# Layer 0's gate projection taken into the attention items by a written TensorE order, and layer 1's modulation sums in two parts

## The chip, the cores and the metric

One core of one Trainium2 chip runs the whole program. The metric is the device time of one execution in microseconds, the median of several runs; lower is better. The engines are TensorE (PE, its weight loads PEld), VectorE (DVE), ScalarE (ACT), GpSimd (POOL) and SyncE (SP, whose queue issues most of the DMAs).

## The reference, cut to what matters

Two layers, 128 context tokens and 512 latent tokens of width 2048. Layer 0 is grouped-query attention with 16 heads of 128 and 4 key/value heads, layer 1 an RG-LRU. Each mixer's output is multiplied by a SiLU gate of the branch's width before its output projection; each layer has a shift, a scale and a gate from `silu(cond) @ w_mod[l]`.

```python
def adaln(cond, w_mod, b_mod):
    m = jax.nn.silu(cond) @ w_mod + b_mod
    shift, scale, gate = jnp.split(m[:, None, :], 3, axis=-1)
    return shift, scale, gate
...
def attn_context(h, w_in, q_norm, k_norm, w_out):
    q, k, v, g = attn_in(h, w_in, q_norm, k_norm)
    o = blocked_attention(q, k, v)
    return (o * jax.nn.silu(g)) @ w_out, k, v
...
    for l in range(DEPTH):
        sh_c, sc_c, ga_c = adaln(c_ctx[None, :], w_mod[l], b_mod[l])
        sh_s, sc_s, ga_s = adaln(c, w_mod[l], b_mod[l])
        hp = rms_norm(y_p, g_pre[l]) * (1.0 + sc_c) + sh_c
        hs = rms_norm(y_s, g_pre[l]) * (1.0 + sc_s) + sh_s
        ...
        y_p = y_p + ga_c * rms_norm(mp, g_post[l])
        y_s = y_s + ga_s * rms_norm(ms, g_post[l])
```

Latent tokens attend to 768 keys (256 cached, 512 own), context tokens to their own 128.

## The kernel before

All large products are float32, split into a high and a low fp32r part (`split_w`: ScalarE casts `wh`, VectorE subtracts to get `wl`), and taken as three matmuls (`mm3`). The split weights live in a ring of three pairs, the raw weights in a pool of four 1 MB tiles (`rawp`). The layer's input stays in SBUF transposed, as `hi` and `lo`, 16 tiles of 644 columns (512 latent tokens, 2 spare, 128 context tokens, 2 spare).

The order of layer 0: first the input and V; then K and four blocks of Q (`gemm_nat`, 4 calls of the background each, then `norm_rope` on VectorE and ScalarE with a write to DRAM); then the gate in 8 blocks of two heads (`gemm_T`), whose result `g_evac` brings from PSUM with a tanh and a multiplication and writes to DRAM as `g_s`; then attention; then the output projection.

Attention runs over 72 items (h, m): for each head four blocks of 128 latent queries, and after every second head one item (h, 4) with the context queries of both. An item has a score part (`stage_s`: 6 matmuls 384 wide into a score tile of PSUM, then maximum, exp, normalization), a part that transposes the probabilities (`stage_t`: 6 transposes and their split into `pth` and `ptl`), and after every second item the product with V (`stage_v`: 18 matmuls). A loop issues the score part of item n, the transposes of item n−3, the product of item n−4 and a piece of the next head's q (`step_q`). There are two score tiles, four probability tiles and two of `pth` and `ptl`. Queries come back from DRAM together with the gate, the product with V is multiplied by the gate and goes straight into `hi` and `lo` for the output projection.

Layer 1's shift and scale come from `gemv`: VectorE multiplies rows of `w_mod` with the conditioning, one column of it per partition, and adds into two accumulators (`ga`, one each for latents and context). It is a generator. Part 0 is the shift, part 1 the scale, each has two halves of 1024 columns, and a half has 8 steps of four sums. Each half ends in a final: split, 8 matmuls with `sel` 512 wide, a copy, 8 transposes. `background()` in each of 36 calls (20 in K/Q, 16 in the gate) adds 32/36 to a credit and takes a step when it has reached one.

A scheduler orders the instructions of each engine by priority in the order of the program, `split_w` ahead of others.

Of the kernel before, what the change touches and what calls it, by code (L numbers as in the profile page):

```python
# [9 lines left out]
F32 = mybir.dt.float32  # L10
# [7 lines left out]
D = 2048  # L18
# [15 lines left out]
AHEAD = 3  # L34
QV = (1, 2, 3)
QO = (2, 2, 3)
PB = 4
# [7 lines left out]
def hybrid_step(ctx: ExitStack, tc: tile.TileContext, i, o):  # L45
# [18 lines left out]
    g_s = [tc.dram_tile([128, TW], F32, name=f"g_s{h}") for h in range(NH)]  # L64
# [314 lines left out]
    def gemv():  # L379
        for part in range(2):  # L380
            for half in range(2):
                acc = [pb.tile([128, 1024], F32, name=f"ga{c}", tag=f"ga{c}") for c in range(2)]
                for kb in range(8):
                    w = rawp.tile([128, 2048], F32, name="raw", tag="raw")
                    w2 = w.rearrange("p (k n) -> p k n", k=2)
                    SY.dma_start(w2, i["w_mod"][1, kb * 256:kb * 256 + 256,
                                                part * D + half * 1024:part * D + half * 1024 + 1024]
                                 .rearrange("(k p) n -> p k n", p=128))
                    for k2 in range(2):
                        k = kb * 2 + k2  # L390
                        for c in range(2):
                            if k == 0:
                                V.tensor_scalar(acc[c], w2[:, k2], cT[:, k, c:c + 1], None, op0=mult)
                            else:
                                V.scalar_tensor_tensor(acc[c], w2[:, k2], cT[:, k, c:c + 1], acc[c],  # L395
                                                       op0=mult, op1=add)
                    yield
                pd_ = psd()
                for c in range(2):
                    ah, al = split_w(acc[c])  # L400
                    for j, x in enumerate((ah, al)):
                        for b in range(2):
                            PE.matmul(pd_[:2, b], sel[:, c], x[:, b * 512:b * 512 + 512], start=(c + j == 0),
                                      stop=(c + j == 2))
                row = pb.tile([2, 2, 512], F32, name="row", tag="row")
                S.copy(row, pd_[:2])
                for k in range(8):
                    PE.transpose(pd_[:, 0, 2 * k:2 * k + 2], row[:, k // 4, (k % 4) * 128:(k % 4) * 128 + 128],
                                 ident[:2, :2])
                kt = half * 8  # L410
                src = pd_[:, 0, :16].rearrange("p (k c) -> p c k", c=2)
                bcol = VA[:, 80 + part * 16 + kt:80 + part * 16 + kt + 8].unsqueeze(1).to_broadcast([128, 2, 8])
                if part == 0:
                    V.tensor_tensor(shift[1][:, kt:kt + 8].rearrange("p k c -> p c k"), src, bcol, op=add)
                else:
                    tmp = small.tile([128, 2, 8], F32, name="gt", tag="gt")
                    V.tensor_tensor(tmp, src, bcol, op=add)
                    gp = VA[:, 16 + kt:16 + kt + 8].unsqueeze(1).to_broadcast([128, 2, 8])
                    V.scalar_tensor_tensor(scale[1][:, kt:kt + 8].rearrange("p k c -> p c k"), tmp, 1.0,
                                           gp, op0=add, op1=mult)  # L420

    gv = gemv()
# [64 lines left out]
    def g_evac(acc, gb):  # L487
        for f in range(2):
            th = pb.tile([128, 2, 512], F32, name="qs", tag="qs", bufs=2)
            gg = pb.tile([128, 2, 512], F32, name="qf", tag="qf", bufs=2)  # L490
            S.activation(th[:, :, :TH], acc[f][:, :, :TH], AF.Tanh, scale=0.5)
            V.scalar_tensor_tensor(gg[:, :, :TH], th[:, :, :TH], 1.0, acc[f][:, :, :TH], op0=add, op1=mult)
            G.dma_start(g_s[gb * 2 + f].rearrange("p (h t) -> p h t", h=2), gg[:, :, :TH])

# [12 lines left out]
    for gb in range(8):  # L507
        g_evac(gemm_T(w_in, 3072 + gb * 256, background), gb)
# [10 lines left out]
    psS = pool("psS", 2, PSUM, stack=xs)  # L519
    psH = pool("psH", 4, PSUM, stack=xs)  # L520

    def pst():
        return psS.tile([128, 2, 512], F32, name="sp", tag="sp")
# [4 lines left out]
    def attn_kv(j):  # L528
        c = slice(j * 128, j * 128 + 128)
        raw = rawp.tile([128, 2048], F32, name="raw", tag="raw")  # L530
        kx = raw[:, :896].rearrange("p (t d) -> p t d", d=128)
        vx = pc_.tile([128, 7, 128], F32, name="vx", tag="vx")
        for x, cache, scr in ((kx, "cache_k", k_s), (vx, "cache_v", v_s)):
            SY.dma_start(x[:, 0:2], i[cache][0, 0, :, j, :].rearrange("(t p) d -> p t d", p=128))
            SY.dma_start(x[:, 2:7], scr[:, c].rearrange("(t p) d -> p t d", p=128))
        kh = pc_.tile([128, 896], F32R, name="kh", tag="kh", bufs=2)
        kl = pc_.tile([128, 896], F32R, name="kl", tag="kl", bufs=2)
        for a, e in ((0, 4), (4, 7)):
            p = psh()
            n = (e - a) * 128  # L540
            for t in range(a, e):
                PE.transpose(p[:, (t - a) * 128:(t - a) * 128 + 128], kx[:, t], ident)
# [3 lines left out]
        return kh, kl, vx  # L546

    def attn_v(j):
        kh, kl, vx = kvs[j]
# [5 lines left out]

    def attn_q(h):

        raw = rawp.tile([128, 2048], F32, name="raw", tag="raw")
        qx = raw[:, :640].rearrange("p (t d) -> p t d", t=5)
        SY.dma_start(qx, q_s[:, h * 128:h * 128 + 128].rearrange("(t p) d -> p t d", p=128))  # L560
        gt = raw[:, 640:640 + TW]
        SY.dma_start(gt, g_s[h])
        qh = ring.tile([128, 1024], F32R, name="wh", tag="wh")
        ql = ring.tile([128, 1024], F32R, name="wl", tag="wl")
        qs_[h] = qh, ql, gt, raw[:, 640 + TW:640 + TW + 512], qx

    def attn_qt(h, a, e):
        qh, ql, _, _, qx = qs_[h]
        p = psh()
        for m in range(a, e):  # L570
            PE.transpose(p[:, (m - a) * 128:(m - a) * 128 + 128], qx[:, m], ident)
        d = slice(a * 128, e * 128)
        n = (e - a) * 128
        S.copy(qh[:, d], p[:, :n])
        V.tensor_tensor(ql[:, d], p[:, :n], qh[:, d].bitcast(F32), op=sub)

    def softmax(sv, n, P, eng):
# [8 lines left out]
        for j in range(n):  # L586
# [3 lines left out]
            elif eng == "p":  # L590
# [454 lines left out]
```

## Time and profile before

| | |
|---|---|
| median of 3 runs | 1954.91 us (1953.88 to 1956.12) |
| profiled execution | 1955.32 us, span 1953.6 us |
| TensorE busy | 1883.5 us, 96% of the span |
| weight loads | 1673.2 us, 86% |
| VectorE busy | 1323.9 us, 68% |
| ScalarE busy | 865.0 us, 44% |
| DMA | 304.20 MB, mean 156 GB/s |

Busy time is what an engine's instructions took; matmuls are pipelined, so a busy TensorE may still lose time between them. The page names the engine that is busy longest, windows of the span tell in which stage the others have room, and the timeline at the borders of the stages tells what one stage hands to the next. Times in the rows below are microseconds from the start of the span.

### The profile page before, as it was taken

What the parts mean: (1) busy time and instruction counts of PE and PEld (TensorE: products, weight loads), DVE (VectorE), ACT (ScalarE), POOL (GpSimd) and SP (SyncE); (2) the same over time, 40 slices, a digit from 0 to 9 for tenths busy, and PEclk for the clock granted to TensorE, in tenths of its full rate; (3) what the DMA queues carried; (4) which work ended last, traced back from release to release, by engine and by line L of the source; (5) the groups of instructions that cost most, each with busy time, mean ns of one, the idle gap of its engine ahead of it and who ended that gap; (6) DMA issues with size and microseconds to landing.
All of it is one profiled execution on the core that took longest, in us unless ns stands there. A gap on an engine that the chain in (4) does not pass through costs nothing.

```text
span 1953.6 us, 26764 instructions
## 1 busy us (share of the span) xinstructions
PE 1883.5 (96%) x10857; PEld 1673.2 (86%) x10857; DVE 1323.9 (68%) x1846; ACT 865.0 (44%) x1255; POOL 133.1 (7%) x212
## 2 busy tenths in 40 slices
PE   4999999999999899999999989899999999999996
PEld 1567887879999899998888889899999999987885
DVE  3237759758375389998857774875685675798645
ACT  4441223222121388881223565666456456742232
POOL 0000000000000001110000000110010010020000
PEclk9999999999999999999999999999999999999998
DMA  9996535536454212225636673323232232546445
GB/s 342 343 318 209 166 109 183 178 123 200 149 178 158 74 38 74 74 97 174 204 130 211 226 263 109 122 77 117 94 102 92 94 100 64 175 140 212 146 149 216
DMA packets 194892, 304.20 MB, mean 156 GB/s; under 512 B 7232, under 2 KB 124608, under 8 KB 191952
## 3 DMA queue, kind: packets, MB, share of 16 engines
q1 hardware_dynamic: 188800, 276.20, 42.6%
q0 software_dynamic: 5968, 26.28, 3.7%
q8 instruction: 85, 1.39, 0.3%
q14 instruction: 39, 0.32, 0.0%
HBM read 273.03 MB, written 29.43 MB: 155 GB/s over the span
## 4 chain that ended last, share of the span: by engine, by line
PE 83%; DVE 6%; ACT 5%; issue 2%; DMA 2%; SPq 1%; POOL 0%; DVEq 0%; ACTq 0%; POOLq 0%
PE pd L184 22%; PE pd L185 22%; PE pd L186 22%; PE pd L215 2%; PE pm L276 2%; PE pd L217 2%; PE pd L218 2%; PE ph L631 1%; PE pg L184 1%; ACT L937 1%; PE pg L186 1%; PE pg L185 1%; PE sp L184 1%; PE sp L186 1%; PE ph L184 1%
## 5 line engine op out<-in xcount | busy, mean ns | idle before, releaser
L179 ACT CAST wh<-raw 128x1024 fp32r<-128x1024 f32 x248 | 258.1, 1048 | 604.8 <-PE pd L186 323.6
L180 DVE TENSOR_TENSOR wl<-raw,wh 128x1024 fp32r<-128x1024 f32 x248 | 301.4, 1221 | 237.5 <-ACT wh L179 236.6
L184 PE MATMUL pd<-wh,hi 128*128 128x512 f32 x1040 | 410.4, 395 | 5.8 <-ACT pd L783 3.3
L185 PE MATMUL pd<-wl,hi 128*128 128x512 f32 x1040 | 409.9, 394 | 0.0
L186 PE MATMUL pd<-wh,lo 128*128 128x512 f32 x1040 | 409.7, 394 | 0.0
L184 PE MATMUL pd<-hi,wh 128*128 128x322 f32 x1280 | 399.2, 312 | 0.0
L186 PE MATMUL pd<-hi,wl 128*128 128x322 f32 x1280 | 397.0, 310 | 1.1 <-DVE wl L180 1.1
L185 PE MATMUL pd<-lo,wh 128*128 128x322 f32 x1280 | 397.5, 311 | 0.0
L186 PEld LDWEIGHTS pd<-hi,wl 128*128 128x128 f32 x1280 | 241.6, 189 | 1.6 <-DVE wl L180 1.6
L185 PEld LDWEIGHTS pd<-lo,wh 128*128 128x128 f32 x1280 | 242.2, 189 | 0.1
L184 PEld LDWEIGHTS pd<-hi,wh 128*128 128x128 f32 x1280 | 241.4, 189 | 0.5 <-ACT wh L179 0.3
L184 PEld LDWEIGHTS pd<-wh,hi 128*128 128x128 f32 x1040 | 195.5, 188 | 52.5 <-ACT pd L783 3.7
L186 PEld LDWEIGHTS pd<-wh,lo 128*128 128x128 f32 x1040 | 195.4, 188 | 45.9
L185 PEld LDWEIGHTS pd<-wl,hi 128*128 128x128 f32 x1040 | 195.4, 188 | 45.4 <-DVE wl L180 0.3
L741 DVE SCALAR_TENSOR_TENSOR ga<-raw,cT,ga 128x512 f32<-128x512 f32 x256 | 175.5, 744 | 15.2 <-DMA ga<-b_mod 12.4
L395 DVE SCALAR_TENSOR_TENSOR ga<-raw,cT,ga 128x1024 f32<-128x1024 f32 x120 | 149.7, 1278 | 28.1 <-DMA raw<-w_mod 27.5
L215 PE MATMUL pd<-hi,wh 128*128 128x256 f32 (+1 forms) x256 | 80.5, 314 | 6.4 <-ACT wh L179 4.7
L184 PE MATMUL pd<-xh,wh 128*128 128x322 f32 x256 | 81.1, 318 | 5.2 <-ACT xh L875 4.4
L185 PE MATMUL pd<-xl,wh 128*128 128x322 f32 x256 | 80.0, 313 | 0.0
L218 PE MATMUL pd<-hi,wl 128*128 128x256 f32 (+1 forms) x256 | 79.9, 312 | 0.0
L217 PE MATMUL pd<-lo,wh 128*128 128x256 f32 (+1 forms) x256 | 79.8, 312 | 0.0
L186 PE MATMUL pd<-xh,wl 128*128 128x322 f32 x256 | 79.8, 312 | 0.0
(233 smaller groups left out, 2807.3 us busy)
## 6 DMA issues: line engine op xcount, KB each, us to landing
raw<-w_mod SPq DMA_DIRECT2D x64, 1024.0 KB, 5.2
raw<-w_in_lru SPq DMA_DIRECT2D x40, 1024.0 KB, 5.3
raw<-w_in_attn SPq DMA_DIRECT2D x36, 1024.0 KB, 6.1
raw<-w_mod SPq DMA_DIRECT2D x64, 512.0 KB, 8.4
raw<-w_out_attn SPq DMA_DIRECT2D x20, 1024.0 KB, 6.0
raw<-w_out_lru SPq DMA_DIRECT2D x20, 1024.0 KB, 5.3
g_s<-qf POOLq DMA_DIRECT2D x16, 322.0 KB, 3.4
raw<-g_s SPq DMA_DIRECT2D x16, 322.0 KB
```

The source lines that it names most:

```text
L179: S.copy(wh, src)
L180: V.tensor_tensor(wl, src, wh.bitcast(F32), op=sub)
L184: PE.matmul(out, ah, bh, start=first, stop=False)
L185: PE.matmul(out, ah, bl, start=False, stop=False)
L186: PE.matmul(out, al, bh, start=False, stop=last)
L215: PE.matmul(outs[f], wh[:, c], hi[:, k, t], start=(k == 0 and first[f]), stop=False, skip_group_check=True)
L217: PE.matmul(outs[f], wh[:, c], lo[:, k, t], start=False, stop=False, skip_group_check=True)
L218: PE.matmul(outs[f], wl[:, c], hi[:, k, t], start=False, stop=(k == KT - 1), skip_group_check=True)
L276: PE.matmul(pm[32 * j:32 * j + 32], c32[:, kb * 4 + j], raw[:, j * 512:j * 512 + 512], start=(kb == 0), stop=(kb == 3))
L395: V.scalar_tensor_tensor(acc[c], w2[:, k2], cT[:, k, c:c + 1], acc[c], op0=mult, op1=add)
L631: PE.transpose(pt[:, c * 128:c * 128 + 128], P[:, b, c * 128:c * 128 + 128], ident)
L741: V.scalar_tensor_tensor(acc[:, c], raw[:, k4 * 512:k4 * 512 + 512], cT[:, kb * 4 + k4, c:c + 1], acc[:, c], op0=mult, op1=add)
```

## The change

The gate is no longer a stage of its own. `gate()` is a generator that issues one matmul per step, head by head, into one PSUM accumulator (`psG2`, one tile of two banks); tanh and multiplication leave the result `gg` in SBUF (four tiles). Under a written order of TensorE, `fill(n)` issues n of these matmuls: 44 ahead of attention (`LEAD`), then 8, 7 and 6 in each item (`FILL`), 21. An item now does scores of n, product of n−2, transposes of n−1. To make room, there is one score tile instead of two, two probability tiles instead of four, one `pth`, `ptl`, `kh`, `kl`. The product with V is multiplied with `gg` in place, written to DRAM per head as `a_s`, and read back and split into `hi` and `lo` by `load_a` after attention's code. `gemv` takes the part as an argument: part 0 runs in K/Q, at a credit of 16/19 in each of 20 calls, part 1 in attention, one step in every second item. Its `yield` stands in the inner loop, and its final is 16 float32 matmuls of 128 by 128 by two columns in place of split, matmuls, copy and transposes. What is left of part 0 after the Q blocks is drained ahead of the gate.

```diff
-    def gemv():
-        for part in range(2):
-            for half in range(2):
...
-                    for k2 in range(2):
-                        k = kb * 2 + k2
-                        for c in range(2):
...
                     yield
+    def gemv(part, p, ps_):
+        for half in range(2):
...
+                for k2 in range(2):
+                    k = kb * 2 + k2
+                    for c in range(2):
...
                     yield
+            pg = ps_()
+            for k in range(8):
                 for c in range(2):
+                    PE.matmul(pg[:, 2 * k:2 * k + 2], acc[c][:, k * 128:k * 128 + 128],
+                              sel[:, c].bitcast(F32), start=(c == 0), stop=(c == 1))
...
-        credit[0] += 32 / 36
+        credit[0] += 16 / 19
...
-    for gb in range(8):
-        g_evac(gemm_T(w_in, 3072 + gb * 256, background), gb)
     for _ in gv:
         pass
...
-    psS = pool("psS", 2, PSUM, stack=xs)
+    psS = pool("psS", 1, PSUM, stack=xs)
     psH = pool("psH", 4, PSUM, stack=xs)
+    psG = pool("psG2", 1, PSUM, stack=xs)
...
+    def gate():
...
+        load(0)
+        split(0, 0)
+        for h in range(NH):
+            if h + 1 < NH:
+                load(h + 1)
+            acc = psG.tile([128, 2, 512], F32, name="pg", tag="pg")
+            for half in range(2):
+                if half == 0:
+                    split(h, 1)
+                elif h + 1 < NH:
+                    split(h + 1, 0)
+                wh, wl = ws.pop((h, half))
+                for k8 in range(8):
...
+                        for n, (x, y) in enumerate(((wh, hi), (wh, lo), (wl, hi))):
+                            PE.matmul(acc[:, e, :TH], x[:, c], y[:, k, t], start=(k == 0 and n == 0),
+                                      stop=(k == KT - 1 and n == 2))
+                            yield
+            gg = pc_.tile([128, TW], F32, name="gg", tag="gg", bufs=4)
+            g2 = gg.rearrange("p (h t) -> p h t", h=2)
+            S.activation(g2, acc[:, :, :TH], AF.Tanh, scale=0.5)
+            V.scalar_tensor_tensor(g2, g2, 1.0, acc[:, :, :TH], op0=add, op1=mult)
+            ggs[h] = gg
+            yield
...
+                y = ggs[h - 1 + e][:, PO:TE]
+                V.scalar_tensor_tensor(y, po[:, e * 128:e * 128 + 128], 0.5, y, op0=mult, op1=mult)
+                G.dma_start(a_s[h - 1 + e][:, :TE], ggs[h - 1 + e][:, :TE])
...
+    with tc.manual_schedule(engines={mybir.EngineType.PE}):
+        load_kv(0)
+        load_q(0)
+        fill(LEAD - 12)
+        attn_k(0)
+        attn_q(0)
+        fill(12)
+        for n in range(len(items) + 2):
...
+                stage_s(it)
+                if it == last[h] and h + 1 < NH:
+                    if h % 4 == 3:
+                        attn_k(h // 4 + 1)
+                    attn_q(h + 1)
+            fill(FILL[0])
+            if n >= 2:
...
+                stage_v((h, m), *done.pop(n - 2))
+            fill(FILL[1])
+            if 0 <= n - 1 < len(items):
+                done[n - 1] = stage_t(items[n - 1])
+            fill(FILL[2])
+            if n % 2:
+                next(gv, None)
...
+    def load_a(k):
+        raw = rawp.tile([128, 2048], F32, name="raw", tag="raw")
+        for e in range(2):
+            r = raw[:, e * TE:e * TE + TE]
+            SY.dma_start(r, a_s[k + e][:, :TE])
+            S.copy(hi[:, k + e, :TE], r)
+            V.tensor_tensor(lo[:, k + e, :TE], r, hi[:, k + e, :TE].bitcast(F32), op=sub)
+    for k in range(0, KT, 2):
+        load_a(k)
```

The order of TensorE's instructions where K/Q ends and the gate begins, before (`pd` is a PSUM accumulator, `sel` picks a column; the last row is the gate's first matmul):

```order
L186 MATMUL pd<-wh,lo 128x512
L403 MATMUL pd<-wh,sel 2x512 x2
L403 MATMUL pd<-wl,sel 2x512 x2
L184 MATMUL pd<-hi,wh 128x322
L185 MATMUL pd<-lo,wh 128x322
```

and with the change (`ga_1294` and `ga_1295` are the accumulators of the sums' half 0, `ga_2990` and `ga_2991` those of half 1):

```order
L184 MATMUL pd<-wh,lo 128x512
L399 MATMUL pd<-sel,ga_1294 128x2
L399 MATMUL pd<-sel,ga_1295 128x2
L399 MATMUL pd<-sel,ga_2990 128x2
L399 MATMUL pd<-sel,ga_2991 128x2
L539 MATMUL pg<-hi,wh 128x322
L539 MATMUL pg<-lo,wh 128x322
```

Of the finals one row of each accumulator stands here; there are 8. The finals of both halves lie between K/Q and the gate. VectorE at the same place, before (from the reduction of the last q block to the gate's first splits):

```order
L463 TENSOR_REDUCE ss<-qs 128x8
L395 SCALAR_TENSOR_TENSOR ga_3008<-raw,cT,ga_3008 128x1024
L155 TENSOR_SCALAR rv<-ss 128x8
L180 TENSOR_TENSOR wl<-raw,wh 128x1024 x3
L414 TENSOR_TENSOR shift_151<-pd,VA 128x2x8
```

and with the change (the last rows; L391 opens part 1's sums):

```order
L393 SCALAR_TENSOR_TENSOR ga_2990<-raw,cT,ga_2990 128x1024
L471 TENSOR_TENSOR qs<-qf,gain_q 128x512
L393 SCALAR_TENSOR_TENSOR ga_2991<-raw,cT,ga_2991 128x1024
L178 TENSOR_TENSOR wl<-raw,wh 128x1024 x2
L178 TENSOR_TENSOR wl<-raw,wh 128x1024
L405 TENSOR_TENSOR shift_151<-pd,VA 128x2x8
L391 TENSOR_SCALAR ga_3291<-raw,cT 128x1024
```

Between the last split of K/Q and the gate's first split (`wl`, here L178) 30 rows of sums (L391, L393) now stand among the normalization; before there was one.

TensorE at a head change of the gate, with the change (`pg` is the gate's accumulator; the number tells one tile from the next, `ph_4244` is a product with V):

```order
L539 MATMUL pg_3941<-hi_118,wl_3943 128x322
L182 MATMUL ph_4244<-pth_4149,vh_3320 128x256
L183 MATMUL ph_4244<-ptl_4150,vh_3320 128x256
L184 MATMUL ph_4244<-pth_4149,vl_3321 128x256
L539 MATMUL pg_4266<-hi_118,wh_4111 128x322
```

and VectorE there (`gg_4241` is the result of the head that has ended, and its multiplication at L545 is what frees `pg_3941`):

```order
L611 TENSOR_REDUCE mx_4227<-sp_4219 128x1
L393 SCALAR_TENSOR_TENSOR ga0_3291<-raw_4653,cT_144,ga0_3291 128x1024
L178 TENSOR_TENSOR wl_4432<-raw_4264,wh_4431 128x1024
L615 RECIPROCAL rs_4229<-sm_4228 128x1
L545 SCALAR_TENSOR_TENSOR gg_4241<-gg_4241,pg_3941 128x644
```

Of 18 matmuls of the product three stand here. Of the 15 head changes two have nothing between the last and the first gate matmul, six have the 18 of a product with V, six have scores and q's transposes (one of them with finals of the sums as well), and one has the six transposes of an item.

The sync queue where attention ends and the output projection begins, before:

```order
L560 DMA raw_7760<-q_s_94 128x5x128
L562 DMA raw_7760<-g_s15_93 128x644
L170 DMA raw_8135<-w_out_attn 128x4x512
L170 DMA raw_8211<-w_mod 128x4x512
```

and with the change:

```order
L739 DMA raw_8078<-a_s13_91 128x642
L739 DMA raw_8085<-a_s14_92 128x642
L168 DMA raw_8106<-w_out_attn 128x4x512
L739 DMA raw_8085<-a_s15_93 128x642
L756 DMA gp_8177<-g_post 128x512
```

The first load of the output projection's weights now stands behind the reload of head 14, whose write comes after the last item of attention.

## Rows read from the trace of the kernel before

**Rows 1.** The page: busy time of each engine, and ScalarE's weight casts.

```profile
PE 1883.5 (96%) x10857; PEld 1673.2 (86%) x10857; DVE 1323.9 (68%) x1846; ACT 865.0 (44%) x1255; POOL 133.1 (7%) x212
...
L179 ACT CAST wh<-raw 128x1024 fp32r<-128x1024 f32 x248 | 258.1, 1048 | 604.8 <-PE pd L186 323.6
```

**Rows 2.** Windows: us, then PE, PEld, DVE, ACT, POOL busy, PEclk, DMA share, GB/s.

```profile
200.00:250.00 50.00, 50.00 (x217) 40.51 (x216) 36.06 (x56) 13.40 (x17) 2.56 (x4) 1.00 0.53 179
500.00:550.00 50.00, 50.00 (x338) 50.00 (x338) 15.25 (x15) 9.98 (x11) 2.06 (x3) 1.00 0.39 132
750.00:800.00 50.00, 49.49 (x374) 47.67 (x373) 45.25 (x100) 43.17 (x98) 7.25 (x5) 1.00 0.24 72
```

**Rows 3.** TensorE's timeline (start, us, instruction): K/Q's end, and narrow fp32 matmuls.

```profile
34.28 1.05 PE L288 MATMUL pm<-sel,row 128*128 128x2 f32 x8 [0.71 <-ACT row L281]
...
428.69 0.62 PE L403 MATMUL pd<-wh,sel 128*2 128x512 f32 x2
...
430.54 0.32 PE L184 MATMUL pd<-hi,wh 128*128 128x322 f32 x1
```

**Rows 4.** VectorE's groups from 150 to 475: count, busy us, mean ns, idle before.

```profile
L395 DVE SCALAR_TENSOR_TENSOR ga<-raw,cT,ga 128x1024 f32<-128x1024 f32 x81 | 101.2, 1278 | 7.8 <-DMA raw<-w_mod 7.4
L180 DVE TENSOR_TENSOR wl<-raw,wh 128x1024 fp32r<-128x1024 f32 x45 | 54.6, 1221 | 43.2 <-ACT wh L179 43.0
L466 DVE TENSOR_TENSOR qf<-qf,rr 128x1024 f32<-128x1024 f32 (+1 forms) x15 | 15.7, 1045 | 0.3
L463 DVE TENSOR_REDUCE ss<-qs 128x8 f32<-128x1024 f32 (+1 forms) x15 | 15.5, 1035 | 5.1 <-ACT qs L460 5.1
L478 DVE TENSOR_TENSOR qs<-qs,t 128x1024 f32<-128x1024 f32 x10 | 12.1, 1215 | 0.0
L476 DVE TENSOR_TENSOR t<-qf,ropeS_q 128x256 f32<-128x256 f32 x32 | 12.1, 417 | 0.0
L471 DVE TENSOR_TENSOR qs<-qf,ropeC_q 128x512 f32<-128x512 f32 x16 | 11.0, 685 | 0.1
```

**Rows 5.** TensorE's timeline: attention's start, a stretch of it, the output projection's start.

```profile
667.39 0.98 PE L542 MATMUL ph<-ident,raw 128*128 128x128 f32 x7
...
676.31 0.69 PE L184 MATMUL sp<-kh,wh 128*128 128x384 f32 x1 [3.79 <-ACT P L584]
...
761.09 0.81 PE L631 MATMUL ph<-ident,P 128*128 128x128 f32 x6
761.66 0.37 PE L184 MATMUL ph<-pth,vh 128*128 128x256 f32 x1
...
763.90 0.34 PE L184 MATMUL sp<-kh,wh 128*128 128x384 f32 x1
...
764.95 0.82 PE L631 MATMUL ph<-ident,P 128*128 128x128 f32 x6
...
884.08 0.39 PE L184 MATMUL pd<-wh,hi 128*128 128x512 f32 x1
```

**Rows 6.** A window behind attention's first long wait, columns as above.

```profile
676.31:681.31 5.00, 5.00 (x17) 4.90 (x18) 3.40 (x5) 2.87 (x6) 1.23 (x1) 0.50 0.31 92
```

**Rows 7.** Lines L491 and L492: duration in ns, least, median, most.

```profile
L491 ACT ACTIVATE qs<-pd x16: 695/709/712, 464.0 to 663.9; 128x644 f32<-128x644 f32 x16
...
L492 DVE SCALAR_TENSOR_TENSOR qf<-qs,pd x16: 814/821/827, 464.9 to 664.7; 128x644 f32<-128x644 f32 x16
```

**Rows 8.** Timeline of one softmax in attention, VectorE and ScalarE.

```profile
777.74 0.96 DVE L581 TENSOR_REDUCE mx<-sp 128x1 f32<-128x768 f32 x1 [0.62 <-PE sp L186]
...
778.81 0.92 ACT L584 ACTIVATE P<-sp,mx 128x768 f32<-128x768 f32 x1
```

**Rows 9.** DMA issues of the whole span: KB each, median us from issue to landing.

```profile
raw<-w_out_attn SPq DMA_DIRECT2D x20, 1024.0 KB, 6.0
...
y_s<-R POOLq DMA_DIRECT2D x16, 321.0 KB, 2.7
```

**Rows 10.** Waits of weight loads, 680 to 885: us in all, times, longest.

```profile
PEld sp L184 <- ACT P L584: 2.2, 4, 1.0
```

More of the change, by code (lines that the diff above doesn't have):

```diff
@@ L33 @@
 NORM = "dadad"
[L34 to L37, printed above, removed]
+LEAD = 44
+FILL = (8, 7, 6)
 GATE2 = (1, 2, 5)
@@ L377, in hybrid_step @@
     pb = pool("pb", 1, stack=xs)
[L379 to L396 removed]
+    def gemv(part, p, ps_):
+        for half in range(2):
+            acc = [p.tile([128, 1024], F32, name=f"ga{c}", tag=f"ga{c}") for c in range(2)]
+            for kb in range(8):
+                w = rawp.tile([128, 2048], F32, name="raw", tag="raw")
+                w2 = w.rearrange("p (k n) -> p k n", k=2)
+                SY.dma_start(w2, i["w_mod"][1, kb * 256:kb * 256 + 256,
+                                            part * D + half * 1024:part * D + half * 1024 + 1024]
+                             .rearrange("(k p) n -> p k n", p=128))
+                for k2 in range(2):
+                    k = kb * 2 + k2
+                    for c in range(2):
+                        if k == 0:
+                            V.tensor_scalar(acc[c], w2[:, k2], cT[:, k, c:c + 1], None, op0=mult)
+                        else:
+                            V.scalar_tensor_tensor(acc[c], w2[:, k2], cT[:, k, c:c + 1], acc[c],
+                                                   op0=mult, op1=add)
@@ L406, in gemv @@
[L406 to L420, printed above, removed]
@@ L422, in hybrid_step @@
-    gv = gemv()
+                    PE.matmul(pg[:, 2 * k:2 * k + 2], acc[c][:, k * 128:k * 128 + 128],
+                              sel[:, c].bitcast(F32), start=(c == 0), stop=(c == 1))
+            kt = half * 8
+            src = pg[:, :16].rearrange("p (k c) -> p c k", c=2)
+            bcol = VA[:, 80 + part * 16 + kt:80 + part * 16 + kt + 8].unsqueeze(1).to_broadcast([128, 2, 8])
+            if part == 0:
+                V.tensor_tensor(shift[1][:, kt:kt + 8].rearrange("p k c -> p c k"), src, bcol, op=add)
+            else:
+                tmp = small.tile([128, 2, 8], F32, name="gt", tag="gt")
+                V.tensor_tensor(tmp, src, bcol, op=add)
+                gp = VA[:, 16 + kt:16 + kt + 8].unsqueeze(1).to_broadcast([128, 2, 8])
+                V.scalar_tensor_tensor(scale[1][:, kt:kt + 8].rearrange("p k c -> p c k"), tmp, 1.0,
+                                       gp, op0=add, op1=mult)
@@ L529, in attn_kv, with fill, load_kv @@
+    gf = gate()
+    def fill(n):
+        for _ in range(n):
+            next(gf, None)
+    kraw, kvs, vs, qraw, qs_, live = {}, {}, {}, {}, {}, {}
+    def load_kv(j):
         c = slice(j * 128, j * 128 + 128)
         raw = rawp.tile([128, 2048], F32, name="raw", tag="raw")
[L531 to L535, printed above, removed]
@@ L554, in attn_v, with load_q @@
         vs[j] = (vh, vl)
+    def load_q(h):
+        qx = pc_.tile([128, 5, 128], F32, name="qx", tag="qx")
+        SY.dma_start(qx, q_s[:, h * 128:h * 128 + 128].rearrange("(t p) d -> p t d", p=128))
+        qraw[h] = qx
     def attn_q(h):
[L558 to L575, printed above, removed]
+        qx = qraw.pop(h)
+        qh = pc_.tile([128, 640], F32R, name="qh", tag="qh", bufs=2)
+        ql = pc_.tile([128, 640], F32R, name="ql", tag="ql", bufs=2)
+        for a, e in ((0, 4), (4, 5)):
+            p = psh()
+            for m in range(a, e):
+                PE.transpose(p[:, (m - a) * 128:(m - a) * 128 + 128], qx[:, m], ident)
+            d = slice(a * 128, e * 128)
+            n = (e - a) * 128
+            S.copy(qh[:, d], p[:, :n])
+            V.tensor_tensor(ql[:, d], p[:, :n], qh[:, d].bitcast(F32), op=sub)
+        qs_[h] = qh, ql
     def softmax(sv, n, P, eng):
@@ L680, in hybrid_step @@
             items.append((h, 4))
+    last = {h: (h, 4 if h % 2 else 3) for h in range(NH)}
     done = {}
-    kvs[0] = attn_kv(0)
-    attn_q(0)
-    attn_qt(0, 0, 4)
-    attn_qt(0, 4, 5)
-    def step_s(n):
-        if n < len(items):
-            stage_s(items[n])
-    def step_t(n):
-        if 0 <= n - AHEAD < len(items):
-            done[n - AHEAD] = stage_t(items[n - AHEAD])
-    def step_v(n):
-        a = n - AHEAD - 1
-        if 0 <= a < len(items):
-            h, m = items[a]
-            if m == 0 and h % 4 == 0:
-                attn_v(h // 4)
-            stage_v((h, m), *done.pop(a))
```

127 lines of the change are left out of this document (54 added, 73 removed).

## The prediction

> **What bounds the kernel now.** I read the page first, then windows of three stages, then TensorE's timeline at the seams between them, then VectorE's groups of instructions. The profiled execution took 1955.32 us with a span of 1953.6, 0.4 us above the median of the runs shown; my sum stands against 1955.32. On the page TensorE is busy for 96% of the span and VectorE for 68% [rows 1], so what counts is where TensorE stands still or loads weights without covering them. In the windows it is busy for all of 50 us in the K/Q projections and in the gate projection, and for 49.49 of 50 in attention, always at a granted clock of 1.00 [rows 2]. The three stages follow each other: K/Q ends at 428.69, the gate's first matmul comes at 430.54, attention's first transpose at 667.39, and the out-projection's first matmul at 884.08 [rows 3, 5]. What lies between 430.54 and 884.08, 453.5 us, is what the change stirs together. VectorE has slack in K/Q (36.06 busy of 50) and in the gate (15.25), little in attention (45.25) [rows 2].
>
> **The change part by part.**
>
> *Finals of the sums.* Each of four ends one half of the shift or scale sums. Two lie at the seam before the gate: one between 428.69 and 430.54, 1.85 us, four rows of two matmuls 512 wide [rows 3]. One leaves K/Q: **−1.9 us**. The new final is 16 fp32 matmuls of two columns; a like group of 8 took 1.05 us [rows 3], so 2 us each.
>
> *The seam after K/Q.* By the order, `yield` now stands inside the loop over k2, so that one call of the generator gives two sums and not four. The 20 calls in K/Q at a credit of 16/19 make 16 steps: 32 sums, half 0 alone. Half 1's 32 sums are issued by the loop that drains the generator, and on VectorE they stand behind the last K/Q split, among the last q group's normalization, and all but the last pair ahead of the gate's first splits; on TensorE the second 16 finals stand ahead of the gate. They cannot begin earlier: the sums' buffers are the ones that the first 16 finals read, and those stand behind the last K/Q matmul. So after K/Q VectorE does 32 sums at 1.25 (one takes 1.278, 101.2/81 = 1.25 with the overlap of neighbours), 40.0 us; the normalization of one of five groups, 15.5/5, 15.7/5, 12.1/5, the rope products 12.1/4 and 11.0/4, 14.4 us; 2 splits at 1.22, 2.4 us [rows 4]. Together 56.8; then the second finals, 2. The gate starts 59 us after K/Q's end: **+59**. Low end 52, with a third of the normalization done ahead of the end; high end 66, with its small instructions and their waits for ScalarE (5.1 in the row of L463) on top.
>
> *TensorE's work in the joined stage.* The gate's 1536 matmuls keep their shape: 338 of them fill 50 us [rows 2], so 227.2. Attention, from the starts of neighbouring rows at full speed [rows 5]: scores 763.90 to 764.95, 1.05; transposes 761.09 to 761.66, 0.57; product with V 761.66 to 763.90, 2.24. 64 x (1.05 + 0.57) + 32 x 2.24 = 175.4; the q and k transposes (108 at about 0.1, from seven in 0.82), 10.8, and the eight items of the prompt, whose tiles are a third as wide (about 1.3 each with all their parts), 10.6: 196.8. Two finals of the sums add 4. Total 428.0 where 453.5 were: **−25.5**. Attention alone now takes 884.08 − 667.39 = 216.7, so this says that the interleaving buys back 20 us of waits and short stalls, at most.
>
> Row and rule part here. TensorE shows 49.49 us busy of 50 in attention, its weight loads 47.67, against 50 of both in the gate [rows 2]. The Trainium skill ("Perfetto Trace Analysis", "Identifying the Most-Contended Engine") calls matmul time a poor measure and weight loads a better one. By that rule attention loses 4.6% of 216.7, 10 us and not 20, and the total would be 10 us higher, 2055; I go by the starts of the rows.
>
> *The clock after the seam.* Before, TensorE once idled for 3.79 us; behind that the granted clock was 0.50, the lower of two levels, from 676.31 to 681.31 [rows 5, 6]. Of 5.0 us at half speed half is lost; after the longer stand I take the like: **+3** (1 to 5).
>
> *The gate's accumulator.* Before, four PSUM tiles let the next projection start while the last was read. Now there is one: at each of 15 head changes the next head's first matmul waits for tanh (0.71) and multiplication (0.82) of the old one [rows 7], about 0.4 for three hand-overs (the exp begins 0.11 after the maximum it needs [rows 8]), and in both queues an instruction ahead: the next split (1.05 and 1.22) [rows 1, 4], or an exp of 0.92 [rows 8]. With the 18 products with V between (2.24 of cover) 4.1 to 4.3 less 2.24, 1.9; 6 boundaries. With scores and q transposes between (1.5) 1.4 to 2.4; 6. With nothing, 3; 2. With finals, none. 6 x 1.9 + 5 x 1.4 + 2.4 + 2 x 3 = **+27**. Low 6.5, if the splits run ahead and only what tanh and multiplication exceed the cover is left; high 55, if every boundary costs 3.7.
>
> *Other waits in the joined stage.* Weights of the gate and K, q loads stand behind eight 1 MB loads of w_mod on the sync queue, one score tile and one P-transposed tile serve where two did, and the items past the gate's end (the filling runs out before the last two) go bare. The trace shows none of this; the 20 us that attention loses with two score tiles is the nearest row, and I take two thirds of it: **+13** (2 to 28).
>
> *The end.* Gated outputs now go to DRAM and come back. For heads 0 to 13 that lies beside the filling. The last pair does not: after the last V product come the multiplication 0.5, the write 3 (321 KB took 2.7), issue 0.5, and since the sync queue holds the reload of head 14 ahead of the first out-projection weights, those only then: 6.0 to land, cast 1.05, split 1.22 [rows 1, 4, 9]. TensorE waits **+12** (7.5 to 17), where nothing was [rows 5], and the clock behind this gap is booked like the one after the seam, **+3** (1 to 5). The gate's own DRAM trip, which goes, was hidden: TensorE had no wait in the gate's stage [rows 2].
>
> Sum: −1.9 + 59 − 25.5 + 3 + 27 + 13 + 12 + 3 = **+89.6**: 1955.3 + 89.6 = 2045. All low ends give 1998, all high ends 2104.
>
> **The rivals.** (1) *The accumulator's waits are cheap*, 6.5 instead of 27: 2024. For it: ScalarE and VectorE had slack in the gate; against: with two score tiles TensorE still waited for the exp, 2.2 us in four waits [rows 10]. The Trainium skill ("TensorE: Matmul & The Clock Gate", "HAM oscillation — how this bites in real kernels") tells of a kernel in which double buffering PSUM gave nothing more. Chance 0.12.
>
> (2) *ScalarE and VectorE set the pace* with one score tile: maximum 0.96, exp 0.92 [rows 8], hand-overs 0.5, with a sum 1.25 and a split 1.22 in the queue, 4.85, against cover of 21 x 0.148 + 0.57 = 3.7. It decides in the items whose stretch of the queue holds both a sum and a split, 36 to 40: 1.2 each, 45, in place of 8 of the other waits: 2045 + 45 − 8 = 2082. Chance 0.13.
>
> (3) *The other side: VectorE is ahead.* If it had 35 of the 40 us of half 1's sums behind it when K/Q ends, the seam costs 2, no clock falls, and with cheap accumulators and no other waits the sum is −1.9 + 2 − 25.5 + 6.5 + 15 = −4: 1951. For it: VectorE's 14 us of slack in 50 of K/Q, some 75 over the stage's 280 [rows 2]. Against: its order, and the first finals that must read the same buffers. The Trainium skill ("Perfetto Trace Analysis", "Optimization Strategy") holds that interleaving stages with different most contended engines may pay. Chance 0.03.
>
> (4) *That the change does not do what it says* is part of the forecast: the sums are not spread over K/Q, and the product of attention, if not the gate, still goes to DRAM and back.
>
> **How the numbers follow.** Forecast 0.70, about 2045. About 0.2%, 4 us, is what a measurement here can tell from none. Faster needs rival 3 whole: 0.03; within 0.2%: 0.01; slower: 0.96, which takes in 0.02 for what no case names. The range reaches to rivals 1 and 2 with some of their own spread: 2012 to 2084.
>
> **What would show it.** Right: after the last K/Q matmul a TensorE gap near 59 us, VectorE full of sums in it, then a clock of 0.50; at head changes the gate's first matmul waiting for the multiplication of the gate, 1 to 3 us each; a gap of 12 us before the out-projection that ends with its weight load. Wrong: a seam under 10 us, or the joined stage from the gate's first matmul to attention's last over 500 us or under 440.

## The result, and the profile of the changed kernel

The changed kernel takes 2069.01 us (median of 4 runs, 2067.38 to 2074.52) against 1954.59 us: a ratio of 1.0586, interval 1.0572 to 1.0600. The forecast of 2045 us had the sign and most of the size; the time lies inside the range (2012 to 2084), 24 us above the forecast. The profiled execution has a span of 2066.5 us, 112.9 more than before. On the page, busy times and the granted clock in 40 slices:

```profile
PE 1908.4 (92%) x10921; PEld 1706.3 (83%) x10921; DVE 1333.9 (65%) x1862; ACT 856.8 (41%) x1235; POOL 111.4 (5%) x196
...
PEclk9999999966999999999899999999999999999998
```

TensorE's share fell from 96% [rows 1], and two slices show a granted clock near 0.6, a third, at the end of attention, one near 0.8 (the last slice shows 0.8 before as well). TensorE's timeline at the seam behind K/Q (start, us, instruction, idle time before and what ended it):

```profile
426.40 3.90 PE L399 MATMUL pd<-sel,ga 128*128 128x2 f32 x32
482.17 0.56 PE L399 MATMUL pd<-sel,ga 128*128 128x2 f32 x2 [51.87 <-DVE ga L393]
483.28 6.56 PE L399 MATMUL pd<-sel,ga 128*128 128x2 f32 x30 [0.55 <-DVE ga L393]
489.70 0.61 PE L539 MATMUL pg<-hi,wh 128*128 128x322 f32 x1
```

K/Q ends at 426.40 and the gate begins at 489.70, 63.3 us where 1.85 were [rows 3]. VectorE's groups in the same stretch, 426.4 to 482.2 (count, busy, mean ns, idle before):

```profile
L393 DVE SCALAR_TENSOR_TENSOR ga<-raw,cT,ga 128x1024 f32<-128x1024 f32 x30 | 36.9, 1276 | 0.0
L457 DVE TENSOR_TENSOR qf<-qf,rr 128x1024 f32<-128x1024 f32 (+1 forms) x3 | 3.1, 1040 | 0.0
...
L391 DVE TENSOR_SCALAR ga<-raw,cT 128x1024 f32<-128x1024 f32 x2 | 1.5, 750 | 3.0 <-PE pd L399 3.0
```

The 32 sums of half 1 all stand there, behind the first finals (the 3.0 of waiting), and VectorE has next to no other idle time (52.78 us busy of 55.80). TensorE's waits from 480 to 1010 (us in all, times, longest):

```profile
PE pg L539 <- DVE gg L545: 29.0, 13, 4.4
PE pd L182 <- ACT wh L177: 10.2, 1, 10.2
PE pg L539 <- DVE rs L615: 3.1, 1, 3.1
PE sp L182 <- ACT P L614: 0.8, 1, 0.8
```

Fourteen of the fifteen head changes wait, 32.1 us, and the single score tile costs 0.8. One head change, from the timeline of ScalarE, VectorE and TensorE:

```profile
546.24 0.31 PE L539 MATMUL pg<-hi,wl 128*128 128x322 f32 x1
...
546.44 1.04 ACT L177 CAST wh<-raw 128x1024 fp32r<-128x1024 f32 x1 [1.57 <-PE pg L539]
547.39 0.70 ACT L544 ACTIVATE gg<-pg 128x644 f32<-128x644 f32 x1
547.52 1.23 DVE L178 TENSOR_TENSOR wl<-raw,wh 128x1024 fp32r<-128x1024 f32 x1
548.66 0.82 DVE L545 SCALAR_TENSOR_TENSOR gg<-gg,pg 128x644 f32<-128x644 f32 x1
...
549.62 0.61 PE L539 MATMUL pg<-hi,wh 128*128 128x322 f32 x1 [3.07 <-DVE rs L615]
550.03 0.47 PE L539 MATMUL pg<-lo,wh 128*128 128x322 f32 x1
```

The cast needs the ring slot that the old head's last matmul frees, so it becomes ready in the same moment as the tanh and stands ahead of it; on VectorE the split (L178) likewise stands ahead of the multiplication that frees the accumulator. Behind the wait a matmul comes every 0.41 and later 0.27 us where it is 0.15 at full clock. Windows of the stage (length, PE, PEld, DVE, ACT, POOL busy, granted clock, DMA):

```profile
494.50:550.00 55.50, 48.16 (x314) 47.29 (x313) 39.72 (x58) 24.86 (x45) 0.00 (x0) 0.93 0.42 124
550.00:600.00 50.00, 45.56 (x304) 45.20 (x304) 28.33 (x49) 18.84 (x39) 1.10 (x2) 0.91 0.30 90
600.00:650.00 50.00, 47.02 (x340) 46.53 (x339) 37.96 (x63) 24.37 (x49) 3.21 (x3) 1.00 0.40 122
...
489.70:983.20 493.50, 459.00 (x3141) 453.30 (x3141) 328.04 (x542) 220.47 (x431) 14.70 (x17) 0.95 0.31 95
```

The same stage of the kernel before, from the gate's first matmul to the output projection:

```profile
430.54:884.08 453.54, 443.08 (x3117) 430.83 (x3117) 325.37 (x557) 230.16 (x456) 41.58 (x39) 0.99 0.36 117
```

At the end of attention, in the timeline of all engines:

```profile
983.82 1.07 POOL L687 DMA_DIRECT2D a_s<-gg  x2 [47.63 <-DVE gg L686]
...
986.63 0.32 SPq L739 DMA_DIRECT2D raw<-a_s  x1
987.05 0.38 SPq L168 DMA_DIRECT2D raw<-w_out_attn  x1
...
992.34 1.99 ACT L177 CAST wh<-raw 128x1024 fp32r<-128x1024 f32 x2 [2.01 <-DMA raw<-w_out_attn]
```

The weight load goes out after the reload of head 14, and the output projection starts at 993.43 where the last product started at 982.92.

Where the 112.9 us are, by TensorE's starts: K/Q −2.3; the seam +61.4; the joined stage to its last product +39.8; the gap behind it +10.4; the rest +3.6, nearly all of it the cold clock of the output projection's first 6 us.

### The profile page after: what moved, and what is told of

Read it like the earlier page. It is cut to its first block, busy times and chain, and to the rows that moved or that the text cites. A ratio compares the mean times of both kernels' runs of the same rounds, so it can differ in the third digit from the quotient of the medians.

```text
span 2066.5 us, 26919 instructions
## 1 busy us (share of the span) xinstructions
PE 1908.4 (92%) x10921; PEld 1706.3 (83%) x10921; DVE 1333.9 (65%) x1862; ACT 856.8 (41%) x1235; POOL 111.4 (5%) x196
## 4 chain that ended last, share of the span: by engine, by line
PE 74%; DVE 8%; issue 7%; ACT 5%; DMA 3%; SPq 1%; POOL 0%; DVEq 0%; ACTq 0%; POOLq 0%
PE pd L182 17%; PE pd L183 17%; PE pd L184 17%; PE pg L539 7%; DVE ga L393 3%; DMA raw<-w_mod 2%; PE pd L213 2%; PE pm L274 2%; PE pd L215 2%; PE pd L216 2%; DVE wl L178 1%; PE ph L656 1%; PE pg L182 1%; ACT L960 1%; PE pg L184 1%
## 5 line engine op out<-in xcount | busy, mean ns | idle before, releaser
L178 DVE TENSOR_TENSOR wl<-raw,wh 128x1024 fp32r<-128x1024 f32 x248 | 301.7, 1221 | 233.6 <-ACT wh L177 232.9
L182 PEld LDWEIGHTS pd<-wh,hi 128*128 128x128 f32 x1040 | 196.0, 189 | 62.0 <-ACT wh L177 10.4
L182 PE MATMUL pd<-hi,wh 128*128 128x322 f32 x768 | 239.6, 312 | 0.0
L183 PE MATMUL pd<-lo,wh 128*128 128x322 f32 x768 | 238.4, 310 | 0.0
L184 PE MATMUL pd<-hi,wl 128*128 128x322 f32 x768 | 238.1, 310 | 0.0
L539 PE MATMUL pg<-hi,wh 128*128 128x322 f32 x512 | 168.2, 328 | 32.0 <-DVE gg L545 29.0
L393 DVE SCALAR_TENSOR_TENSOR ga<-raw,cT,ga 128x1024 f32<-128x1024 f32 x120 | 150.8, 1279 | 26.7 <-DMA raw<-w_mod 26.7
L539 PE MATMUL pg<-lo,wh 128*128 128x322 f32 x512 | 166.6, 325 | 0.0
L539 PE MATMUL pg<-hi,wl 128*128 128x322 f32 x512 | 162.9, 318 | 0.0
L183 PEld LDWEIGHTS pd<-lo,wh 128*128 128x128 f32 x768 | 145.3, 189 | 0.0
L184 PEld LDWEIGHTS pd<-hi,wl 128*128 128x128 f32 x768 | 145.0, 189 | 0.0
L539 PEld LDWEIGHTS pg<-hi,wh 128*128 128x128 f32 x512 | 100.5, 196 | 34.8 <-issue 34.8
L539 PEld LDWEIGHTS pg<-lo,wh 128*128 128x128 f32 x512 | 100.8, 197 | 0.0
```

Source lines behind the costliest of these rows:

```text
L178: V.tensor_tensor(wl, src, wh.bitcast(F32), op=sub)
L182: PE.matmul(out, ah, bh, start=first, stop=False)
L183: PE.matmul(out, ah, bl, start=False, stop=False)
L184: PE.matmul(out, al, bh, start=False, stop=last)
L539: PE.matmul(acc[:, e, :TH], x[:, c], y[:, k, t], start=(k == 0 and n == 0), stop=(k == KT - 1 and n == 2))
```

## The experiments

The kernels below start from the changed one unless said otherwise. Ratios stand to the kernel before, on the same chip. On the chips used, that kernel's median was 1953.7 to 1956.3 us, so a difference in us between runs on different chips can be off by about 2.5.

**The seam.**

```diff
-        credit[0] += 16 / 19
+        credit[0] += 32 / 19
```

> The changed kernel with one edit: the background's credit per call is 32/19 in place of 16/19, so that all 32 steps of part 0 fall into K/Q. Theory (the 63 us between K/Q and the gate are sums that the halved step size left over): the stand shrinks to about 4 to 6 us (finals and the last normalization) and the cold clock behind it goes; 2069 - 60 = 2009 us, range 2002 to 2016. Rival (VectorE has no room for 32 more sums in K/Q, they turn into waits of TensorE there or at the gate's start): 2040 us or more.

Measured: 2028.38 us, 1.0373 (1.0356 to 1.0391), 41 under the changed kernel. The sums fit into K/Q, which ends 3.7 us later with a narrow final now inside it, and the 52 us wait is gone, so the rival falls, but 19 us of the gain are missing. TensorE's timeline behind K/Q, which ends at 430.08, and one row of ScalarE's:

```profile
445.88 0.90 PE L573 MATMUL ph<-ident,raw 128*128 128x128 f32 x3 [5.33 <-ACT qs L451]
453.22 0.44 PE L182 MATMUL sp<-kh,qh 128*128 128x384 f32 x1 [2.36 <-ACT qh L603]
458.23 0.69 PE L184 MATMUL sp<-kh,ql 128*128 128x384 f32 x1 [4.40 <-DVE ql L604]
...
445.23 0.60 ACT L451 ACTIVATE qs<-pd 128x512 f32<-128x512 f32 x1 [4.13 <-DMA q_s<-qs]
```

Twelve us of new waits: the last Q block's PSUM tiles, VectorE and ScalarE are not free yet when attention, now 44 matmuls after K/Q and no longer 237 us, asks for them; from 450 to 500 the granted clock is 0.82. In the changed kernel the long stand (the time in which TensorE stood waiting for the sums) had hidden that.

**The gate's accumulator.** Each head in two token halves with a one-bank tile each, the loop over `e` outside:

```diff
-            acc = psG.tile([128, 2, 512], F32, name="pg", tag="pg")
+            for e in range(2):
+                acc = psG.tile([128, 512], F32, name=f"pg{e}", tag=f"pg{e}")
...
+                S.activation(gg[:, t], acc[:, :TH], AF.Tanh, scale=0.5)
+                V.scalar_tensor_tensor(gg[:, t], gg[:, t], 1.0, acc[:, :TH], op0=add, op1=mult)
```

> The changed kernel with one edit: each head's gate is computed in two token halves, each with its own one-bank PSUM tile, so that tanh and multiplication of one half run beside the 48 matmuls of the other; instruction shapes of TensorE stay. The seam stays as it is. Theory (about 34 us of waits at 14 head changes, and about 20 us of lowered clock behind those of over 3 us): the waits shrink to almost nothing and the windows from 500 to 950 show a granted clock of 1.00; 2069 - 50 = 2019 us, range 2012 to 2030. Rival (ScalarE and VectorE set the pace of the joined stage, the wait reappears at the one score tile): 2050 to 2069 us.

Measured: 2032.71 us, 1.0392 (1.0374 to 1.0409), 36 less. The two longest of TensorE's seven groups of waits from 490 to 950, and two windows:

```profile
PE sp L182 <- ACT P L616: 4.0, 3, 2.9
PE ph L183 <- DVE ptl L662: 1.0, 1, 1.0
```

```profile
550.00:600.00 50.00, 50.00 (x359) 49.90 (x358) 35.33 (x62) 25.63 (x53) 1.10 (x2) 1.00 0.37 111
...
700.00:750.00 50.00, 47.11 (x326) 46.68 (x325) 41.79 (x65) 22.76 (x46) 3.23 (x3) 0.93 0.48 147
```

No wait for the accumulator is left, and from 550 to 900 the clock is 1.00 in every window of 50 us but this second one. Two things stand in it, a narrow final of the sums without a wait and a score that waits for an exp, and a stretch at 0.50 follows each:

```profile
702.61 3.63 PE L399 MATMUL ph<-sel,ga 128*128 128x2 f32 x32
...
740.47 0.58 PE L182 MATMUL sp<-kh,qh 128*128 128x384 f32 x1 [2.89 <-ACT P L616]
```

```profile
706.47:709.88 3.41, 3.41 (x14) 3.41 (x13) 3.18 (x5) 0.00 (x0) 0.00 (x0) 0.50 0.31 127
740.60:744.02 3.42, 3.42 (x13) 3.32 (x14) 2.80 (x5) 0.62 (x2) 0.00 (x0) 0.50 0.40 162
```

The rival, ScalarE and VectorE as the pace, falls. In the joined stage itself 41 us are gone (452.4 against 493.3, by TensorE's starts), while K/Q took 3 us more in the profiled execution, where a copy of V held up its start for 3.8 us and not 1.6. The missing 9 are in part the 7.5 us of waits that remain, the 4.0 at the score tile among them; the rest is the clock, which gave back about 13 us and not 20, since the stretches behind the seam and behind the narrow finals stayed. The Trainium skill ("Perfetto Trace Analysis", "Matmuls") says that independent groups of matmuls should rotate through PSUM banks, so that the evacuation of one lies beside the next. These two runs agree, with 36 us for it.

**The end.** Heads 14 and 15 go straight into `hi` and `lo`:

```diff
-                G.dma_start(a_s[h - 1 + e][:, :TE], ggs[h - 1 + e][:, :TE])
+                if h < NH - 1:
+                    G.dma_start(a_s[h - 1 + e][:, :TE], ggs[h - 1 + e][:, :TE])
+                else:
+                    y, z = ggs[h - 1 + e][:, :TE], hi[:, h - 1 + e, :TE]
+                    S.copy(z, y)
+                    V.tensor_tensor(lo[:, h - 1 + e, :TE], y, z.bitcast(F32), op=sub)
...
-    for k in range(0, KT, 2):
+    for k in range(0, KT - 2, 2):
```

> The changed kernel with one edit: heads 14 and 15 go from SBUF straight into hi and lo, without the trip through DRAM. Theory (the 10.5 us before the output projection are the trip and the weight load queued behind its reload, plus 3 us of cold clock): 2069 - 12 = 2057 us, range 2054 to 2060. Rival (the weight load waits for a free tile or for bandwidth anyway): 2065 us or more.

Measured: 2056.56 us, 1.0517 (1.0495 to 1.0539), 12.4 less, as expected; in its trace the output projection's first matmul comes at 985.98, right behind the last product's at 985.86.

**All three.**

> The three edits together. Theory (three separate places, the gains add: 60 + 50 + 12): 2069 - 122 = 1947 us, range 1938 to 1960, which is about 0.4% under the kernel before, because the interleaving itself buys about 20 us of attention's waits. Rival (the interleaving buys nothing, or VectorE becomes the limit once the stands are gone): 1965 us or more.

Measured: 1978.45 us, 1.0119 (1.0099 to 1.0138). The gains add: 41 + 36 + 12 = 89 of the 90.6 found. The theory that the places are separate holds; that the interleaving then makes the kernel faster than before does not, and the time lies where the rival put it (1965 or more). In windows at the end of K/Q:

```profile
432.02:436.40 4.38, 4.38 (x34) 4.38 (x33) 0.49 (x3) 1.77 (x2) 0.00 (x0) 0.81 0.39 101
436.40:439.40 3.00, 3.00 (x12) 3.00 (x13) 2.94 (x6) 0.00 (x0) 0.00 (x0) 0.50 0.00 0
```

TensorE is never idle here. In the first stretch it does one narrow final, and behind it the gate runs at 0.50.

**More gate ahead of attention** (on the last one):

```diff
-LEAD = 44
-FILL = (8, 7, 6)
+LEAD = 140
+FILL = (7, 7, 6)
```

> The kernel of e4_all with 140 gate matmuls ahead of attention in place of 44, and 20 per item in place of 21. Theory (what is left of the seam are about 12 us of waits and some 10 us of lowered clock between 443 and 465, because attention's first transposes, scores and PSUM tiles wait for the last q block's normalization on VectorE, which the gate stage used to cover): 96 matmuls more, 14 us, cover it; 1978 - 18 = 1960 us, range 1953 to 1968. Rival (the waits are set by loads behind the sync queue, so they come as late as before): 1972 us or more.

Measured: 1976.63 us, 1.0112 (1.0090 to 1.0134): no change. The time is in the rival's range, but not for the rival's reason: the wait moved to the first head change, whose multiplication on VectorE stands behind the same normalization, which ends at 449.2, and behind part 1's first sums (a row of TensorE and two of VectorE):

```profile
455.50 0.63 PE L543 MATMUL pg<-hi,wh 128*128 128x322 f32 x1 [6.39 <-DVE gg L547]
...
450.44 4.60 DVE L393 SCALAR_TENSOR_TENSOR ga<-raw,cT,ga 128x1024 f32<-128x1024 f32 x2
454.97 0.48 DVE L547 SCALAR_TENSOR_TENSOR gg<-gg,pg 128x322 f32<-128x322 f32 x1
```

**The finals** (on the last one, part 0 with the old code, part 1 cut by `yield` after each two of its eight columns; and on the kernel before, the new code alone).

> e5_lead with part 0's finals as in the kernel before (512 wide, then transposes) and part 1's narrow finals cut into four pieces over four items. Theory (a narrow final is 32 passes, 3.6 to 4.4 us at full clock, after which the granted clock was 0.50 for about 5 us without any idle time before): four finals give back 2 us each and four cold stretches 2.5 each; e5_lead less 14 us, range less 8 to less 18. Rival (the clock fell for the wait at the seam and not for the narrow matmuls): less than 5 us.

> The kernel before with one part of the change alone: the narrow float32 finals in place of the 512-wide ones, at the same places. Theory (narrow finals cost 2 us more each and cool the clock): 1955 + 14 = 1969 us, range 1960 to 1975, with a granted clock under 1.00 behind each. Rival (a final saves the split, the copy and the transposes and is no slower): 1950 to 1957 us.

Measured: 1963.56 us, 1.0056 (1.0038 to 1.0073), 13 less than the one above; and for the kernel before with narrow finals 1965.95 us, 1.0056 (1.0039 to 1.0073). So the finals alone slow the kernel before by 11 to 12 us. There they stand between full matmuls without a gap, one row and the window around it:

```profile
299.11 3.63 PE L401 MATMUL pd<-sel,ga 128*128 128x2 f32 x32
```

```profile
300.00:325.00 25.00, 25.00 (x116) 20.74 (x115) 20.80 (x27) 6.54 (x9) 0.00 (x0) 0.93 0.37 126
```

and the same window of the kernel before:

```profile
300.00:325.00 25.00, 25.00 (x114) 19.15 (x113) 23.48 (x31) 10.52 (x13) 0.00 (x0) 1.00 0.71 250
```

The rival, a clock that falls only for waits, is out: here TensorE was busy for all of 25 us, and the clock was 0.93 against 1.00 in the same window of the kernel before.

**Sums later, and a third buffer for the squares.** Part 1's sums from item 9 on (counted from 0), part 0 at 32/18; the second run also with three buffers of `qs` in K/Q.

> The kernel of e6_finals with two edits: part 1's sums begin at the ninth item of attention, and part 0's steps go at 32/18 per call, so that its last final is issued ahead of the last K/Q block. Theory (what is left between 430 and 470 are 2.6 us for the final's transposes, 4.3 us of a head change whose multiplication stood behind sums on VectorE, 4 us of scores behind a sum that waited for its load, and the cold clock behind them): e6_finals less 14 us, 1964 - 14 = 1950 us, range 1943 to 1957, no slower than the kernel before. Rival (the last q block's normalization alone holds VectorE and ScalarE until about 450, so the waits stay): 1959 us or more.

> e7_later with three buffers in place of two for the squares in K/Q's normalization. Theory (ScalarE stood 3 us behind a write of the second buffer to DRAM, and the gate's first tanh behind it): 0 to 3 us less than e7_later. Rival (VectorE's normalization is what ScalarE waits for in the end): equal to e7_later.

Measured: 1.0027 (1.0016 to 1.0038) and 1.0030 (1.0018 to 1.0043), medians 1961.57 and 1960.64. By the ratios (1.0056 before these edits), about 6 of the 14 us came of the first edits, with intervals that leave 2 to 10, and nothing of the third buffer, so the rivals are nearer: the last normalization still held the first head change, 5.0 us in the first trace and 3.4 in the second. In the second trace a narrow final now stands alone behind attention, since the sums ran out of items:

```profile
883.89 6.82 PE L414 MATMUL ph<-sel,ga 128*128 128x2 f32 x32
```

**Sums denser, and the last Q block in two groups.** The first run takes a step in two of three items and gives the projections three buffers; the second adds

```diff
-    def norm_rope(acc, nm, dst, extra=None):
-        for a, ms in zip(acc, PAIRS):
+    def norm_rope(acc, nm, dst, extra=None, pairs=PAIRS):
+        for a, ms in zip(acc, pairs):
...
-        norm_rope(gemm_nat(w_in, n * 512, background), "q", q_s[:, n * 512:n * 512 + 512])
+        for grp in ([PAIRS] if n < 3 else LAST):
+            norm_rope(gemm_nat(w_in, n * 512, background, grp), "q", q_s[:, n * 512:n * 512 + 512], None, grp)
```

> e7b_qs3 with two edits: from the ninth item on two items in three take a step of part 1's sums, so that its last final falls inside attention and not behind it, and the projections' copies have three buffers. Theory (in the trace of e7b_qs3 the last narrow final stood alone at the end, 30 passes in 6.4 us, then a cold clock, and a copy of V waited for a write to DRAM at the start of K/Q, 3.9 us and a cold clock): e7b_qs3 less 12 us, 1961 - 12 = 1949 us, range 1943 to 1956, so 0.0 to 0.6% under the kernel before. Rival (VectorE, with more sums per item, holds up the scores): 1958 us or more.

> e8_dense with the last block of Q taken in two groups of token tiles, the first of which is normalized while the second is computed. Theory (behind K/Q, VectorE's 17 us of normalization hold the gate's first tanh and multiplication, and TensorE waits 3.7 us at the first head change): e8_dense less 5 us, range less 2 to less 9. Rival (weights loaded twice delay the last block by as much): equal to e8_dense or slower.

Measured: 1955.97 us, 1.0004 (0.9994 to 1.0015), no different from the kernel before, and some 5 us less than the run before it where 12 were expected; and 1950.44 us, 0.9974 (0.9959 to 0.9988), 5.5 less than the first, as expected. The wait at the first head change, 3.8 us in the first trace, is not in the second. The last kernel is faster than both kernels, by 0.3% and 6%. TensorE's seam in it, and its joined stage as one window:

```profile
428.05 0.40 PE L184 MATMUL pd<-wh,lo 128*128 128x512 f32 x1
428.29 0.31 PE L561 MATMUL pg<-hi,wh 128*128 128x322 f32 x1
```

```profile
428.29:876.41 448.12, 438.60 (x3141) 433.81 (x3140) 337.19 (x584) 227.25 (x456) 19.06 (x21) 1.00 0.37 116
```

## Why the prediction was right, and where its sum was off

*The finals of K/Q.* Forecast −1.9, measured −2.3 in K/Q, but the price of a new final was misread. I took the eight rows of [rows 3] for eight matmuls. A final of 16 matmuls gives 32 records, so a record is half a matmul, and a narrow final costs 3.6 us at full clock and not 2, 7.5 at the lowered clock of the seam.

*The seam.* Right in place, cause and size: 59 forecast, 63.3 found. VectorE's work kept TensorE until 482.17, 55.8 us after K/Q's end (forecast 56.8): 52.8 us of work, less than forecast, and 3.0 of waiting for the first finals, which had no term, so that two errors cancel there; the rest of the difference is the second finals, 7.5 instead of 2. The run with the other credit shows that the step size is the cause. It returned 41 of the 63 us, since 12 us of waits and a cold clock had been hidden under the stand. The sum also takes off only one of the two old finals that stood ahead of the gate: with the 1.85 us of the old seam off as well, its term is 57 where 61.4 was found.

*The clock behind the seam and behind the end.* 3 each forecast; 0.50 until 494.4 behind the first, 2.4 lost, and 3 in the output projection.

*The joined stage.* This is the step that was mis-sized: 471 us forecast (428.0 of work, 27 for the accumulator, 13 for other waits, 3 for the clock), 493 found. By the window, TensorE stands for 493.50 − 459.00 = 34.5 us, less than the 40 forecast: the accumulator's part is 32.1, more than its 27, and the others 2.4 in place of 13, two errors that partly cancel. The lowered clock costs about 20 us, of which 3 were forecast: it stood at 0.50 in ten stretches of the stage, in which TensorE was busy for 41 us in all, and half of that is lost. I had booked a lowered clock for two stops and none for the fifteen small ones. Seven of the ten stretches begin in or right behind a wait of 1.8 to 4.4 us at a head change, while the windows from 600 to 700, with waits of 1.3 to 1.7 alone, show 1.00. One stretch is the rest of the seam's, and two stand behind narrow finals of part 1's sums, where TensorE did not wait at all; here is one of them:

```profile
722.09 3.63 PE L399 MATMUL ph<-sel,ga 128*128 128x2 f32 x32
```

```profile
726.57:729.98 3.41, 3.41 (x14) 3.41 (x13) 3.41 (x7) 0.99 (x2) 0.00 (x0) 0.50 0.00 0
```

Without the waits for the accumulator, in the second experiment, the clock over the stage came back from 0.95 to 0.98. The work, forecast at 428, was about 7 us more.

*What interleaving can give.* −25.5 forecast, as an upper bound. Before, the stage held 453.54 − 443.08 = 10.5 us of standing and, at 0.99, up to 4.5 of lowered clock: 15 in all, and the best kernel got 5.4 of them (448.1 against 453.5, at a clock of 1.00 and with 9.5 us of standing). The floor of 428 was too low by about 7. Counted by the usual distance from one matmul to the next of its kind in the changed kernel's trace (1536 of the gate at 0.148, 600 of the product at 0.120, 384 of the scores at 0.175 and 48 narrow ones at 0.112, 508 transposes at 0.109, 64 records of finals at 0.112) the work is 434.5. Half of the difference is the finals, 7.2 us and not 4. Most of the rest is a reading of the transposes: I took six of them as 0.57, to the start of the matmul behind them. In the changed kernel:

```profile
964.51 0.82 PE L656 MATMUL ph<-ident,P 128*128 128x128 f32 x6
965.08 0.39 PE L539 MATMUL pg<-hi,wh 128*128 128x322 f32 x1
965.31 0.31 PE L539 MATMUL pg<-lo,wh 128*128 128x322 f32 x1
965.46 0.31 PE L539 MATMUL pg<-hi,wl 128*128 128x322 f32 x1
```

The first gate matmul starts early and the second one 0.23 later, where 0.15 is usual. From the first transpose to the second gate matmul are 0.80 us, which is six times 0.109 and once 0.148: six transposes take 0.65, and the change of kind itself costs nothing.

The rule of the Trainium skill that the prediction weighed ("Perfetto Trace Analysis", "Identifying the Most-Contended Engine"), weight loads as the better measure, was read off one window of 50 us [rows 2], which gave 10 us for attention and 15.5 for this term. Over the whole of attention in the kernel before it gives more, 216.69 − 199.68 = 17 us, near the 20 of the starts of rows:

```profile
667.39:884.08 216.69, 208.41 (x1542) 199.68 (x1541) 189.51 (x409) 177.65 (x396) 28.60 (x20) 0.98 0.23 72
```

Neither measure foretold that only 5.4 us would come. That the 2055 of the rule lies nearer to 2069 is luck, since what was missing is mainly the clock.

*The end.* 12 forecast, 10.5 found; its parts were the ones named, and leaving out the trip returned 12.4 with the cold clock.

*The rivals.* Cheap accumulators did not come: 32.1 us. ScalarE and VectorE did not set the pace: the score tile cost 0.8. VectorE was not ahead at the seam. What the chances missed is a rival that was not listed, short waits, and narrow finals, that cost the clock as well.

## What to carry to other kernels

A generator that is moved between stages keeps its number of steps only if its `yield` stays at the same loop: count what one step gives, and what is left for the drain. A stage that is taken away also takes away the time in which the stage before it finished its work on the other engines; here the last normalization then stood in front of attention, and it took several repairs until it did not. A repeated wait of a few microseconds on TensorE should be priced with the clock behind it, and two half tiles in place of one whole remove it at no cost in PSUM.

## What was not expected of the hardware

Narrow float32 matmuls (128 by 128 by two columns, 113 ns a record) were followed by a lowered clock without any idle time of TensorE: 0.50 behind 4.4 us of them, and 0.93 over the 25 us around 3.6 us of them, though the engine shows as busy throughout. Of the four such finals in the kernel before, three were followed by 3.4 us at 0.50 (from 304.04, 433.75 and 566.87); behind the fourth, which ends at 671.3, the clock was 1.00. In the last kernel, where part 1's finals are cut into pieces of 8 records, the clock was not lowered between 150 and 876. No run here separates the two columns from the float32. Four such finals in the kernel before cost 11 to 12 us, where by busy time (3.63 against 1.85 for the old final's matmuls) they would cost 7 without counting the transposes that they save; half of the 10 us at 0.50 is another 5.
